# One 512-column matmul for both activation halves in the stages without meta tokens

## The chip, the cores and the metric

The kernel runs on one core of one Trainium2 chip. The metric is the device time of one execution in microseconds, the median over several runs. All arithmetic counts as float32: the answer has to hold float32 accuracy, and the kernel reaches that with matmuls of split operands, described below.

## What is computed

One encoder layer over 272 positions (16 learned meta tokens ahead of 256 real ones) of width 2048. It is a half-weighted SwiGLU, then a mixer whose single input projection feeds differential attention and a state-space scan, then an output projection, then a second half-weighted SwiGLU. The meta positions are dropped at the end, so everything behind the keys, the values and the scanned inputs is needed for the 256 real positions alone.

```
def _swiglu(h, w_gate, w_up, w_down):
    return (jax.nn.silu(h @ w_gate) * (h @ w_up)) @ w_down
...
        h = h + 0.5 * _swiglu(_rmsnorm(h, ffn1_norm[l]), ffn1_w_gate[l], ffn1_w_up[l], ffn1_w_down[l])
        u = _rmsnorm(h, mix_norm[l]) @ w_in[l]
...
        h = h + jnp.concatenate([attn, ssd.astype(attn.dtype)], axis=-1) @ w_out[l]
        h = h + 0.5 * _swiglu(_rmsnorm(h, ffn2_norm[l]), ffn2_w_gate[l], ffn2_w_up[l], ffn2_w_down[l])
    return h[:, N_META:]
```

## The kernel before

The residual stream stands transposed in SBUF, features on partitions, tokens along the row. Weights come in 648 tiles of 128 x 1024 float32 (512 KB) in the order of their use. ScalarE (ACT) rounds a tile to `hi` (L154), VectorE (DVE) makes the remainder `lo` (L156), both in the fp32r format that TensorE (PE) reads at one column a cycle. Four buffers hold split tiles; splitting runs three tiles ahead of use. The activations are split in the same way into `yh` and `yl` (or `gh`, `gl` inside the SwiGLU).

A product is three matmuls: `hi`x`yh` (L197), `hi`x`yl` (L198), `lo`x`yh` (L199), in the helper `mm3`, each of which loads its own stationary 128 x 128 weight block and streams the tokens past it. The three add up in the same columns of one PSUM bank. `project(t0)` makes four chunks of 128 output columns from eight weight tiles: per tile it goes through the four chunks, and in each through the tile's two blocks. With `t0 = 0` a matmul has 272 columns, with `t0 = META` it has 256.

Without meta tokens run: the gate and up projections of the second SwiGLU (22 calls of `project(META)`), the projections of the gate z and of the queries (two calls each) and the output projection `w_out_part` (eight groups of four weight tiles; the first four take the scan's half, the last four the attention's). The down projection of the second SwiGLU (`evac2`, L986 to L988) has the activations stationary and streams the weights, 512 columns in a matmul.

The results leave PSUM by an eviction behind each group. Five banks serve as `acc` tiles in turn, and a group takes four, so chunk c of a group stands in a bank until its eviction, and chunk c + 1 of the next group needs that bank. In the second SwiGLU the eviction of the gate is one DVE multiplication (L356), that of the up projection another (L366). Between the weight tiles `step()` and `need()` issue the rest of the mixer (norms, scan, attention) from a queue; a list scheduler then fixes each engine's order.

Of the kernel before, what the change touches and what calls it, by code (L numbers as in the profile page):

```python
# [17 lines left out]
P = 128  # L18
# [29 lines left out]
# columns of w_in  # L48
# [3 lines left out]
def _plan():  # L52
    """The weight tiles in the order of their use: (weight, first row, rows / 128, first column, columns)."""
# [26 lines left out]
# token tiles of the keys and of the scanned positions  # L80
# [4 lines left out]
def hymba_block(ctx: ExitStack, tc: tile.TileContext, h0, pars, consts, dtw, wts, out):  # L85
# [28 lines left out]
    class Lazy(dict):  # L114
        """Slots taken when first asked for."""
# [84 lines left out]

    def project(t0):
        """Four 128-column chunks of y @ w, transposed: [columns, tokens from t0]."""
        accs = [acc_tile() for _ in range(4)]
        for kt in range(KC // 2):
            hi, lo = wtile()
            for c in range(4):
                for k in range(2):
                    kc = 2 * kt + k
                    mm3(accs[c][:, 0:T - t0], hi[:, k, c * P:(c + 1) * P], lo[:, k, c * P:(c + 1) * P],
                        yh[:, kc, t0:T], yl[:, kc, t0:T], kc == 0, kc == KC - 1)  # L210
            step()
        return [a[:, 0:T - t0] for a in accs]

# [22 lines left out]
    # the clock of the tensor engine and the first table of the activation engine, before the data is there  # L236
# [6 lines left out]
    def pc(i):  # L243
        return pcol[:, i:i + 1]

# [1 line left out]
    yh = cp.tile([P, KC, T], F32R, name="yh")  # L247
    yl = cp.tile([P, KC, T], F32R, name="yl")
# [3 lines left out]
    def new_y(kc, wcol, t0, sums):  # L252
        """From the new chunk of h: the halves of h * w, and its share of the sum of squares."""
# [11 lines left out]
    def rsqrt(v, s, r):  # L265
        """r = 1 / sqrt(v): a first guess from the exponent's bits, then Newton steps; s is scratch, v is lost."""
# [8 lines left out]
    def rstd_of(v, width, r):  # L275
        """v: sums of squares, a column per tile of tokens; r = 1 / sqrt(mean + eps)."""
# [805 lines left out]
```

## Time and profile before

| | |
|---|---|
| time, median of 3 runs | 1986.74 us (1984.13 to 1987.38) |
| profiled execution, first to last instruction | 1980.9 us |
| median minus the profiled span | 5.8 us |
| PE busy | 1973.0 us, 15034 matmuls |
| DVE busy | 1103.0 us |
| ACT busy | 894.1 us |
| mean granted TensorE clock | 1.000 (2.4 GHz) |

The profile comes from one execution; of that one only the span is listed, and what lies around it is taken from the difference to the runs' median. PE's busy time counts a matmul from its start to its modelled end; neighbours overlap, so the pace of PE is read from start to start, not from the mean duration.

### The profile page before, as it was taken

The page shows a single profiled execution, that of the slowest core. Times are in us where ns is not written, and L with a number is a line of the kernel's source. Part 1 is how long each engine was busy: PE and PEld are TensorE (multiplying, and loading weights), DVE is VectorE, ACT ScalarE, POOL GpSimd, SP SyncE. Part 2 cuts the span into 40 slices and gives each one's busy share as a digit, 9 for nine tenths or more (in the row PEclk, how much of TensorE's full clock was granted, in tenths as well). Part 3 has the DMA queues.
Part 4 walks back from the last instruction along what each step waited for, and adds up shares of the span by engine and source line. Part 5 has one row for each costly group of instructions (what it writes and reads, how often), then busy time and mean ns, then how long its engine had stood idle before and what let it go on. Part 6 is the DMA issues. An engine that isn't in the chain of part 4 may idle for free.

```text
span 1980.9 us, 36104 instructions
## 1 busy us (share of the span) xinstructions
PE 1973.0 (100%) x15034; PEld 1904.1 (96%) x15034; DVE 1103.0 (56%) x1762; ACT 894.1 (45%) x1311; POOL 25.2 (1%) x61
## 2 busy tenths in 40 slices
PE   9999999999999999999999999999999999999999
PEld 9999999999999999999998889999999889999987
DVE  7545455454545456776866666555555544555554
ACT  6443443334343444456645665544444334444432
POOL 0000000000000000000021000000000000000000
PEclk9999999999999999999999999999999999999999
DMA  7455554544555555464465225455555555555563
GB/s 275 171 175 177 172 180 171 179 172 175 179 181 178 174 178 171 153 217 169 154 194 177 107 107 188 169 186 181 186 186 190 194 191 187 186 182 186 186 215 125
DMA packets 98324, 352.74 MB, mean 178 GB/s; under 512 B 11680, under 2 KB 11728, under 8 KB 98160
## 3 DMA queue, kind: packets, MB, share of 16 engines
q1 hardware_dynamic: 94464, 342.02, 49.5%
q0 software_dynamic: 2544, 6.33, 1.1%
q8 instruction: 117, 1.92, 0.4%
q10 hardware_dynamic: 1152, 2.10, 0.3%
q14 instruction: 47, 0.39, 0.1%
HBM read 347.18 MB, written 3.21 MB: 177 GB/s over the span
## 4 chain that ended last, share of the span: by engine, by line
PE 97%; DVE 1%; DMA 1%; ACT 1%; issue 0%; SPq 0%; POOL 0%; DVEq 0%; ACTq 0%
PE acc L197 27%; PE acc L199 27%; PE acc L198 27%; PE acc L987 4%; PE acc L988 4%; PE acc L986 4%; PE ps L743 1%; ACT hi L154 0%; PE ps L628 0%; DMA u<-k_d 0%; DVE lo L156 0%; DMA raw<-in_wts_dram 0%; PE ps L799 0%; PE ps L802 0%; PE ps L765 0%
## 5 line engine op out<-in xcount | busy, mean ns | idle before, releaser
L156 DVE TENSOR_TENSOR lo<-raw,hi 128x1024 fp32r<-128x1024 f32 x648 | 792.7, 1224 | 732.5 <-ACT hi L154 729.3
L154 ACT CAST hi<-raw 128x1024 fp32r<-128x1024 f32 x648 | 681.7, 1052 | 991.1 <-PE acc L198 770.0
L197 PE MATMUL acc<-yh,hi 128*128 128x272 f32 (+1 forms) x3520 | 1007.9, 286 | 0.8 <-DVE u L648 0.7
L199 PE MATMUL acc<-yh,lo 128*128 128x272 f32 (+1 forms) x3520 | 1001.7, 285 | 0.4 <-DVE lo L156 0.4
L198 PE MATMUL acc<-yl,hi 128*128 128x272 f32 (+1 forms) x3520 | 1001.2, 285 | 0.0
L197 PEld LDWEIGHTS acc<-yh,hi 128*128 128x128 f32 x3520 | 661.8, 188 | 5.0 <-issue 2.0
L199 PEld LDWEIGHTS acc<-yh,lo 128*128 128x128 f32 x3520 | 662.2, 188 | 2.2 <-issue 1.2
L198 PEld LDWEIGHTS acc<-yl,hi 128*128 128x128 f32 x3520 | 661.9, 188 | 1.6 <-issue 1.2
L199 PE MATMUL acc<-u,lo 128*128 128x272 f32 (+1 forms) x960 | 277.3, 289 | 0.0
L197 PE MATMUL acc<-u,hi 128*128 128x272 f32 (+1 forms) x960 | 277.2, 289 | 0.0
L198 PE MATMUL acc<-u,hi 128*128 128x272 f32 (+1 forms) x960 | 275.9, 287 | 0.0
L199 PEld LDWEIGHTS acc<-u,lo 128*128 128x128 f32 x960 | 181.8, 189 | 2.1 <-issue 1.4
L198 PEld LDWEIGHTS acc<-u,hi 128*128 128x128 f32 x960 | 181.8, 189 | 1.0 <-issue 0.4
L197 PEld LDWEIGHTS acc<-u,hi 128*128 128x128 f32 x960 | 181.5, 189 | 1.0 <-issue 0.4
L988 PE MATMUL acc<-lo,u 128*128 128x512 f32 x352 | 137.0, 389 | 0.0
L987 PE MATMUL acc<-hi,u 128*128 128x512 f32 x352 | 137.0, 389 | 0.0
L986 PE MATMUL acc<-hi,u 128*128 128x512 f32 x352 | 136.9, 389 | 0.0
L986 PEld LDWEIGHTS acc<-hi,u 128*128 128x128 f32 x352 | 66.1, 188 | 13.7
L987 PEld LDWEIGHTS acc<-hi,u 128*128 128x128 f32 x352 | 66.1, 188 | 13.7
L988 PEld LDWEIGHTS acc<-lo,u 128*128 128x128 f32 x352 | 66.1, 188 | 13.7
L366 DVE TENSOR_TENSOR u<-acc,u 128x272 f32<-128x272 f32 (+1 forms) x88 | 33.9, 427 | 30.9 <-PE acc L199 30.9
L356 DVE TENSOR_TENSOR u<-acc,rm 128x256 f32<-128x256 f32 (+1 forms) x84 | 33.1, 429 | 31.4 <-PE acc L199 31.4
(266 smaller groups left out, 708.8 us busy)
## 6 DMA issues: line engine op xcount, KB each, us to landing
raw<-in_wts_dram SPq DMA_DIRECT2D x648, 512.0 KB, 3.3
u<-a_d POOLq DMA_DIRECT2D x4, 512.0 KB, 7.7
out_dram<-hx ACTq DMA_DIRECT2D x8, 256.0 KB, 4.7
hx<-in_h_dram SPq DMA_DIRECT2D x7, 272.0 KB, 7.4
u<-k_d POOLq DMA_DIRECT2D x4, 272.0 KB, 7.5
u<-in_consts_dram POOLq DMA_DIRECT2D x1, 472.0 KB, 4.8
hx<-in_h_dram SPq DMA_DIRECT2D x1, 280.0 KB, 2.9
rope<-u POOLq DMA_DIRECT2D x4, 68.0 KB, 2.5
```

The lines of the kernel that those rows point to most:

```text
L154: nc.scalar.copy(hi, raw)
L156: nc.vector.tensor_tensor(lo, raw, hi.bitcast(F32), ALU.subtract)
L197: nc.tensor.matmul(ps, st_hi, mv_hi, start=first, stop=False)
L198: nc.tensor.matmul(ps, st_hi, mv_lo, start=False, stop=False)
L199: nc.tensor.matmul(ps, st_lo, mv_hi, start=False, stop=last)
L356: nc.vector.tensor_tensor(sg[:, c, :], pg[c], rm[:, t0:T], ALU.mult)
L366: nc.vector.tensor_tensor(sg[:, c, :], pu[c], sg[:, c, :], ALU.mult)
L743: nc.tensor.matmul(pss[s], qT[h // 4][r, h % 4, j * P:(j + 1) * P], kT[h // 4][r, h % 4, 0:kw], start=True, stop=True)
L986: nc.tensor.matmul(accs[j], a, hi[:, k, :], start=first, stop=False)
L987: nc.tensor.matmul(accs[j], b_, hi[:, k, :], start=False, stop=False)
L988: nc.tensor.matmul(accs[j], a, lo[:, k, :], start=False, stop=last)
```

## The change

Where there are no meta tokens, the halves `yh` and `yl` (one tile `y` of two rows for each block now; also `oo` and `zz` for the output projection) are streamed by one matmul of 512 columns against `hi`: columns 0 to 255 of the bank get `hi`x`yh`, columns 256 to 511 `hi`x`yl`. A second matmul adds `lo`x`yh` to the columns 256 to 511. The two halves of the bank are added when they are read: `join` copies the upper half to SBUF on ACT, and adds the lower half on DVE. What a DVE instruction did on reading the bank is now done behind it in SBUF. In the attention half of the output projection each half of the bank is added to the residual by its own DVE addition.

```
+    def mm2(ps, st_hi, st_lo, mv, first, last):
+        nc.tensor.matmul(ps, st_hi, mv, start=first, stop=False)
+        nc.tensor.matmul(ps[:, SEQ:2 * SEQ], st_lo, mv[:, 0, :], start=False, stop=last)
...
+                    if t0:
+                        mm2(accs[c], *w, y[:, kc, :, t0:T], kc == 0, kc == KC - 1)
+                    else:
+                        mm3(accs[c][:, 0:T], *w, yh[:, kc, :], yl[:, kc, :], kc == 0, kc == KC - 1)
...
+    def join(dst, ps):
+        nc.scalar.copy(dst, ps[:, SEQ:2 * SEQ])
+        nc.vector.tensor_tensor(dst, ps[:, 0:SEQ], dst, ALU.add)
...
-    yh = cp.tile([P, KC, T], F32R, name="yh")
-    yl = cp.tile([P, KC, T], F32R, name="yl")
+    y = cp.tile([P, KC, 2, T], F32R, name="y")
+    yh, yl = y[:, :, 0, :], y[:, :, 1, :]
...
+                if t0:
+                    for c in range(4):
+                        join(sg[:, c, :], pg[c])
+                        pg[c] = sg[:, c, :]
...
+                if t0:
+                    us = [row_tmp(SEQ) for _ in range(4)]
+                    for c in range(4):
+                        join(us[c], pu[c])
+                    pu = us
...
+        if wi == 0:
+            for c in range(4):
+                join(dst[g][:, c, :], pj[c])
...
-    zh, zl = Lazy([P, 4, SEQ], F32R), Lazy([P, 4, SEQ], F32R)
+    zz = Lazy([P, 2, 2, SEQ], F32R)
...
-                    mm3(accs[c][:, 0:SEQ], hi[:, k, c * P:(c + 1) * P], lo[:, k, c * P:(c + 1) * P],
-                        hs[i // 4][:, i % 4, :], ls_[i // 4][:, i % 4, :], i == 0, i == 7)
+                    mm2(accs[c], hi[:, k, c * P:(c + 1) * P], lo[:, k, c * P:(c + 1) * P],
+                        src[i // 2][:, i % 2], i == 0, i == 7)
...
-            nc.vector.tensor_tensor(t, accs[c][:, 0:SEQ], rz, ALU.mult)
+            join(t, accs[c])
             ts.append(t)
+        for t in ts:
+            nc.vector.tensor_tensor(t, t, rz, ALU.mult)
...
-            nc.vector.tensor_tensor(h, h, accs[c][:, 0:SEQ], ALU.add)
+            for k in range(2):
+                nc.vector.tensor_tensor(h, h, accs[c][:, k * SEQ:(k + 1) * SEQ], ALU.add)
```

The order of PE, first change: two blocks of one weight tile for one chunk, in the first tile of an up projection of the second SwiGLU, before.

```order
L197 MATMUL acc_14960<-yh,hi_14966 128x256
L198 MATMUL acc_14960<-yl,hi_14966 128x256
L199 MATMUL acc_14960<-yh,lo_14968 128x256
L197 MATMUL acc_14960<-yh,hi_14966 128x256
L198 MATMUL acc_14960<-yl,hi_14966 128x256
L199 MATMUL acc_14960<-yh,lo_14968 128x256
```

The same of the changed kernel (the numbers behind the names differ between the two programs).

```order
L204 MATMUL acc_13960<-y,hi_13988 128x512
L205 MATMUL acc_13960<-y,lo_13990 128x256
L204 MATMUL acc_13960<-y,hi_13988 128x512
L205 MATMUL acc_13960<-y,lo_13990 128x256
```

Six matmuls of 256 columns have become two of 512 and two of 256; the sequence of chunks and tiles is the same.

The order of DVE, second change: the end of that up projection before, where the four `acc` tiles are its four chunks in turn, L156 is the split of a weight tile, L366 reads the bank and L368 makes `gl`.

```order
L156 TENSOR_TENSOR lo_15148<-raw_15114,hi_15146 128x1024
L366 TENSOR_TENSOR u_14951<-acc_14960,u_14951 128x256
L156 TENSOR_TENSOR lo_15178<-raw_15144,hi_15176 128x1024
L368 TENSOR_TENSOR u_15205<-u_14951,u_15204 128x256
L366 TENSOR_TENSOR u_14951<-acc_14961,u_14951 128x256
L366 TENSOR_TENSOR u_14951<-acc_14962,u_14951 128x256
L366 TENSOR_TENSOR u_14951<-acc_14963,u_14951 128x256
L156 TENSOR_TENSOR lo_15226<-raw_15174,hi_15224 128x1024
```

The same place of the changed kernel; L227 is the addition of `join`, L390 the multiplication that was L366, now without a bank, L392 the former L368.

```order
L156 TENSOR_TENSOR lo_14122<-raw_14096,hi_14120 128x1024
L227 TENSOR_TENSOR t_14142<-acc_13960,t_14142 128x256
L227 TENSOR_TENSOR t_14143<-acc_13961,t_14143 128x256
L227 TENSOR_TENSOR t_14144<-acc_13962,t_14144 128x256
L390 TENSOR_TENSOR u_13943<-t_14142,u_13943 128x256
L390 TENSOR_TENSOR u_13943<-t_14143,u_13943 128x256
L390 TENSOR_TENSOR u_13943<-t_14144,u_13943 128x256
L227 TENSOR_TENSOR t_14145<-acc_13963,t_14145 128x256
L392 TENSOR_TENSOR u_14141<-u_13943,u_14140 128x256 x3
L390 TENSOR_TENSOR u_13943<-t_14145,u_13943 128x256
L156 TENSOR_TENSOR lo_14174<-raw_14118,hi_14172 128x1024
```

The read of the first chunk's bank has moved behind the weight split that it stood ahead of, and the three multiplications have come in between the reads of the third and of the fourth bank.

On ACT at that place of the changed kernel the copies of `join` (L226) stand between two roundings of weight tiles (L154); before there was no instruction of ACT that read these banks.

```order
L154 CAST hi_14120<-raw_14096 128x1024
L226 COPY t_14142<-acc_13960 128x256
L226 COPY t_14143<-acc_13961 128x256
L226 COPY t_14144<-acc_13962 128x256
L154 CAST hi_14172<-raw_14118 128x1024
L226 COPY t_14145<-acc_13963 128x256
L391 CAST u_14140<-u_13943 128x256 x3
```

Up to the projections without meta tokens (z, some 880 us into the run) the order of all matmuls is that of before.

## Rows read from the trace of the kernel before

**Rows 1.** The page: busy time by engine; granted clock by slice.

```profile
PE 1973.0 (100%) x15034; PEld 1904.1 (96%) x15034; DVE 1103.0 (56%) x1762; ACT 894.1 (45%) x1311; POOL 25.2 (1%) x61
...
PEclk9999999999999999999999999999999999999999
```

**Rows 2.** The page: chain of work that ended last, by engine.

```profile
PE 97%; DVE 1%; DMA 1%; ACT 1%; issue 0%; SPq 0%; POOL 0%; DVEq 0%; ACTq 0%
```

**Rows 3.** Waits of PE alone: total us, times, longest.

```profile
PE ps L239 <- DVE ones L216: 1.1, 1, 1.1
PE acc L197 <- DVE u L648: 0.7, 1, 0.7
PE acc L199 <- DVE lo L156: 0.4, 1, 0.4
```

**Rows 4.** Timeline of PE, 256 columns: first and last of 19 consecutive matmuls.

```profile
1700.08 0.29 PE L197 MATMUL acc<-yh,hi 128*128 128x256 f32 x1
...
1702.22 0.28 PE L197 MATMUL acc<-yh,hi 128*128 128x256 f32 x1
```

**Rows 5.** Timeline of PE, 272 columns: first and last of 19 consecutive matmuls.

```profile
600.03 0.29 PE L197 MATMUL acc<-yh,hi 128*128 128x272 f32 x1
...
602.29 0.29 PE L197 MATMUL acc<-yh,hi 128*128 128x272 f32 x1
```

**Rows 6.** Timeline of PE, 512 columns: first and last of 22 consecutive matmuls.

```profile
1515.05 0.39 PE L986 MATMUL acc<-hi,u 128*128 128x512 f32 x1
...
1519.81 0.39 PE L986 MATMUL acc<-hi,u 128*128 128x512 f32 x1
```

**Rows 7.** Windows of the second SwiGLU: us, busy by engine (count), clock, DMA, GB/s.

```profile
1250.00:1500.00 250.00, 250.00 (x2106) 250.00 (x2105) 129.20 (x152) 107.94 (x133) 0.00 (x0) 1.00 0.54 186
1520.00:1630.00 110.00, 110.00 (x487) 91.06 (x487) 53.49 (x47) 43.12 (x41) 0.00 (x0) 1.00 0.55 194
```

**Rows 8.** Groups by line and shape: matmuls of 256 columns (count, busy, mean ns).

```profile
L197 PE MATMUL acc<-yh,hi 128*128 128x256 f32 x1664 | 470.1, 283 | 0.0
L198 PE MATMUL acc<-yl,hi 128*128 128x256 f32 x1664 | 467.4, 281 | 0.0
L199 PE MATMUL acc<-yh,lo 128*128 128x256 f32 x1664 | 467.0, 281 | 0.0
...
L197 PE MATMUL acc<-u,hi 128*128 128x256 f32 x256 | 73.8, 288 | 0.0
```

**Rows 9.** Groups by line and shape: splits, evictions, and an ACT copy from PSUM.

```profile
L156 DVE TENSOR_TENSOR lo<-raw,hi 128x1024 fp32r<-128x1024 f32 x648 | 792.7, 1224 | 732.5 <-ACT hi L154 729.3 <-PE ps L784 1.8
...
L366 DVE TENSOR_TENSOR u<-acc,u 128x256 f32<-128x256 f32 x44 | 16.6, 419 | 15.2 <-PE acc L199 15.2
...
L942 DVE TENSOR_TENSOR hx<-hx,acc 128x256 f32<-128x256 f32 x16 | 6.1, 418 | 5.5 <-PE acc L199 5.5
...
L807 ACT COPY u<-ps 128x256 f32<-128x256 f32 x8 | 3.0, 376 | 0.0
```

**Rows 10.** Timeline of DVE at the end of an up projection.

```profile
1278.68 0.42 DVE L366 TENSOR_TENSOR u<-acc,u 128x256 f32<-128x256 f32 x1 [1.38 <-PE acc L199]
1279.03 1.21 DVE L156 TENSOR_TENSOR lo<-raw,hi 128x1024 fp32r<-128x1024 f32 x1
1280.16 0.42 DVE L368 TENSOR_TENSOR u<-u,u 128x256 fp32r<-128x256 f32 x1
1280.49 1.08 DVE L366 TENSOR_TENSOR u<-acc,u 128x256 f32<-128x256 f32 x3
```

**Rows 11.** Timeline of ACT at the same place.

```profile
1277.85 1.05 ACT L154 CAST hi<-raw 128x1024 fp32r<-128x1024 f32 x1 [1.80 <-PE acc L198]
...
1280.75 1.05 ACT L154 CAST hi<-raw 128x1024 fp32r<-128x1024 f32 x1 [1.20 <-PE acc L198]
1281.71 1.01 ACT L367 CAST u<-u 128x256 fp32r<-128x256 f32 x3
```

**Rows 12.** Windows of the mixer, columns as in rows 7.

```profile
943.00:1000.00 57.00, 57.00 (x480) 53.08 (x479) 51.31 (x150) 39.09 (x100) 2.26 (x4) 1.00 0.45 153
...
1116.00:1128.00 12.00, 12.00 (x103) 12.00 (x103) 10.01 (x31) 7.54 (x16) 0.00 (x0) 1.00 0.48 177
...
1176.00:1190.00 14.00, 13.96 (x118) 13.75 (x117) 11.11 (x29) 8.96 (x17) 0.00 (x0) 1.00 0.34 122
```

**Rows 13.** Waits of all engines: those of the weight roundings for their transfers.

```profile
ACT hi L154 <- DMA raw<-in_wts_dram: 2.4, 6, 0.9
```

More of the change, by code (lines that the diff above doesn't have):

```diff
@@ L208, in project @@
                     kc = 2 * kt + k
-                    mm3(accs[c][:, 0:T - t0], hi[:, k, c * P:(c + 1) * P], lo[:, k, c * P:(c + 1) * P],
-                        yh[:, kc, t0:T], yl[:, kc, t0:T], kc == 0, kc == KC - 1)
+                    w = hi[:, k, c * P:(c + 1) * P], lo[:, k, c * P:(c + 1) * P]
+                    if t0:
+                        mm2(accs[c], *w, y[:, kc, :, t0:T], kc == 0, kc == KC - 1)
+                    else:
+                        mm3(accs[c][:, 0:T], *w, yh[:, kc, :], yl[:, kc, :], kc == 0, kc == KC - 1)
             step()
-        return [a[:, 0:T - t0] for a in accs]
+        return accs if t0 else [a[:, 0:T] for a in accs]
+    def join(dst, ps):
+        nc.scalar.copy(dst, ps[:, SEQ:2 * SEQ])
+        nc.vector.tensor_tensor(dst, ps[:, 0:SEQ], dst, ALU.add)
     ones = cp.tile([P, P], F32, name="ones")
@@ L644, in qk_evac @@
         sqs = []
+        if wi == 0:
+            for c in range(4):
+                join(dst[g][:, c, :], pj[c])
+            pj = [dst[g][:, c, :] for c in range(4)]
         for c in range(4):
-            sq = row_tmp(pj[c].shape[1])
-            nc.scalar.activation(sq, pj[c], AF.Square)
-            nc.vector.tensor_scalar(dst[g][:, c, :], pj[c], pc(R_QN + wi), None, ALU.mult)
+            p = pj[c]
+            sq = row_tmp(p.shape[1])
+            nc.scalar.activation(sq, p, AF.Square)
+            nc.vector.tensor_scalar(dst[g][:, c, :], p, pc(R_QN + wi), None, ALU.mult)
             sqs.append(sq)
@@ L818, in o_norm @@
                 nc.scalar.activation(O[g][:, j, c, :], O[g][:, j, c, :], AF.Copy, scale=orr[:, 4 * j + c:4 * j + c + 1])
-    oh, ol = Lazy([P, 4, SEQ], F32R), Lazy([P, 4, SEQ], F32R)
+    oo = Lazy([P, 2, 2, SEQ], F32R)
     def o_turn(h):
@@ L826, in o_turn @@
             nc.tensor.transpose(ps[:, j * P:(j + 1) * P], O[g][:, j, c, :], ident)
-        a, b_ = oh[g][:, c, :], ol[g][:, c, :]
+        a, b_ = oo[h // 2][:, h % 2, 0, :], oo[h // 2][:, h % 2, 1, :]
         nc.scalar.activation(a, ps[:, 0:SEQ], AF.Copy, scale=an8)
@@ L844, in attend, with z_a @@
             later(0.45, o_turn, h, label=f"o{h}")
-    zh, zl = Lazy([P, 4, SEQ], F32R), Lazy([P, 4, SEQ], F32R)
+    zz = Lazy([P, 2, 2, SEQ], F32R)
     zss = cp.tile([P, SEQ], F32, name="zss")
     zs = Lazy([P, 4, SEQ])
-    def z_a(ps, ch):
+    def z_a(ch):
         t = zs[ch // 4][:, ch % 4, :]
-        nc.vector.tensor_tensor(t, ps, rm[:, META:T], ALU.mult)
+        nc.vector.tensor_tensor(t, t, rm[:, META:T], ALU.mult)
         nc.scalar.activation(t, t, AF.Silu)
@@ L860, in z_b @@
         nc.vector.tensor_tensor(t, t, xs[g][:, c, META:T], ALU.mult)
-        a, b_ = zh[g][:, c, :], zl[g][:, c, :]
+        a, b_ = zz[ch // 2][:, ch % 2, 0, :], zz[ch // 2][:, ch % 2, 1, :]
         nc.scalar.activation(a, t, AF.Copy, scale=pc(R_SSD + ch))
@@ L873, in hymba_block @@
         for c in range(4):
-            z_a(pj[c], 4 * g + c)
+            join(zs[g][:, c, :], pj[c])
+        for c in range(4):
+            z_a(4 * g + c)
     later(2.4, ssd_exp, 0)
@@ L911, in hymba_block, with w_out_part @@
     zv, zr = small("zv", 2), small("zr", 2)
-    def w_out_part(hs, ls_):
+    def w_out_part(src):
         accs = [acc_tile() for _ in range(4)]
@@ L926, in hymba_block @@
     for dg in range(4):
-        accs = w_out_part(zh, zl)
+        accs = w_out_part(zz)
         need("rz")
@@ L938, in hymba_block @@
     for dg in range(4):
-        accs = w_out_part(oh, ol)
+        accs = w_out_part(oo)
         for c in range(4):
             h = hT[:, 4 * dg + c, META:T]
-            nc.vector.tensor_tensor(h, h, accs[c][:, 0:SEQ], ALU.add)
+            for k in range(2):
+                nc.vector.tensor_tensor(h, h, accs[c][:, k * SEQ:(k + 1) * SEQ], ALU.add)
         for c in range(4):
```

## The prediction

> **What bounds the kernel now.** I read the page's engine totals first: PE is busy all through, in all 40 slices at the full granted clock [rows 1]. The chain that ended last is 97% PE [rows 2]. So a nanosecond taken from PE's stream of matmuls comes off the end, and one added anywhere else costs only if PE comes to wait for it. The list of PE's own waits shows how little it waits: 1.1 us at the start, 0.7 us once for an eviction of the queries, 0.4 us once for a weight split [rows 3]. Neither bank releases nor weights hold it in the second SwiGLU.
>
> PE is not simply at one column per cycle, though. From start to start, 256 columns take (1702.22 - 1700.08) / 18 = 118.9 ns [rows 4], 272 columns 2.26 / 18 = 125.6 ns [rows 5], 512 columns 4.76 / 21 = 226.7 ns [rows 6]. At the granted 2.4 GHz the columns alone are 106.7, 113.3 and 213.3 ns. What is left over is 12.2, 12.2 and 13.3 ns: a price for each matmul that hardly depends on its size. Long stretches bear the two paces out: 250 us / 2106 = 118.7 ns and 110 us / 487 = 225.9 ns [rows 7].
>
> **The change, term by term.** There are 1664 + 256 = 1920 triples of 256 columns [rows 8]: 22 x 64 = 1408 in the second SwiGLU, 256 for z and q, 256 in the output projection. The columns streamed stay the same (768 a triple), but three matmuls become two.
>
> *Term 1, PE.* A triple takes 3 x 118.9 = 356.7 ns. As 512 + 256 it takes 226.7 + 118.9 = 345.6 ns. The difference is 11.1 ns, over 1920 triples 21.3 us. The one price in this that no row shows: for 1664 triples the 512 columns lie in two rows of 256 with 16 columns between them, while the matmuls of rows 6 read 512 in one piece (as `zz` and `oo` will). The lower bound is the 226.7 ns of one piece, the upper two matmuls of 256, 237.8 ns, at which those triples gain nothing and 2.8 us remain from the output projection. I take the lower end: rows 4 to 6 charge by the instruction and its columns, and this is one instruction of 512 columns. Both ends stay in the range.
>
> The Trainium skill, TensorE: Matmul & The Clock Gate, section "Wait — 56ns, not 53.3ns?", states a fixed cost of about 2.5 ns for a warm matmul. By that figure alone the estimate would be 1920 x 2.5 = 4.8 us instead of 21.3. The measured 12.2 ns disagrees with it, and the measurement decides.
>
> *Term 2, joins.* In 26 projections and four groups of the output projection each chunk gets an ACT copy and a DVE addition of 256 columns: 30 x 4 = 120 of each, priced by the ACT copy of that shape at 376 ns (45 us on ACT) and by DVE's eviction at 419 ns (50 us on DVE) [rows 9]. The attention half of the output projection gets 16 more DVE additions at 418 ns, 6.7 us. All of it lies beside PE: in the second SwiGLU's gate and up stretch DVE is busy 129.2 of 250 us and ACT 107.9 [rows 7]. Per projection of 22 us it adds 4 x 0.42 = 1.7 us to DVE and 4 x 0.38 = 1.5 us to ACT. I cost it at nothing there, if the banks come free in time.
>
> *Term 3, the banks.* That is the one wait that the change can create. Put 0 at the start of the weight rounding in the last tile of a projection (1277.85, when PE has let go of the tile before) [rows 11]. Before, the first chunk was read at 1278.68, so at +0.83 [rows 10]. In the new order rounding, copies, and on DVE split and additions follow each other. The split begins at +1.18 (1279.03) and the next DVE instruction at +2.31 (1280.16). The copies on ACT (from about +0.96, as 1281.71 follows 1280.75) hide under it. So the additions begin at +2.31 and, at a spacing of 1.08 / 3 = 0.36 and 0.42 each, let banks one to three go at about +2.7, +3.1 and +3.5. PE's tile takes 8 x 345.6 = 2.76 us; the next projection's second chunk, which needs bank one, starts at about 2.76 + 0.69 = +3.4, its third at +4.1, its fourth at +4.8. The margins are 0.7, 1.0 and 1.3 us. Bank four is not needed for another whole projection, so the rounding and the three multiplications ahead of its read cost nothing. The DVE split that now comes later (L156 behind ten short operations, about +6.5 instead of +5.2) is for a tile used at about 4 x 2.76 = +11.1. If the cover were gone, each us past the margin would cost 1 us at each of 22 projections.
>
> In the attention half of the output projection two additions for each bank put the first bank at about +2.9 and the second at +4.0, against the same +3.4 and +4.1: just in time, and four groups at 0.2 us are under 1 us. Around z, q and the scan's half of the output projection DVE is busy 51.3 of 57, 10.0 of 12 and 11.1 of 14 us [rows 12], with the scan and the attention in front of the evictions. There I bound the loss between 0 and 0.5 us at each of 8 groups, so 0 to 4 us. The 0.7 us wait of rows 3 stays about as it is: the queries' first three banks are now read ahead of the key scaling that held DVE, but the fourth chunk's squares stand behind it.
>
> *Term 4, the weights.* A tile is used up in 2.76 us instead of 2.85, so 190 GB/s. The down projection already draws 194 GB/s [rows 7], and in the whole run roundings waited 2.4 us for transfers [rows 13]. Nothing.
>
> *Sum.* 1980.9 - 21.3 + 1.0 (for term 3) = 1960.6 us of span. What lies around the span is taken as unchanged, 5.8 us between this span and the median of the three runs; so 1966.4 us, 1.0% less.
>
> **The rivals.**
> *A. The two-row read is charged as two reads.* For it: no row shows such a read. Against it: the price per matmul is the same from 256 to 512 columns. It gives 1986.7 - 2.8 + 1 = 1985; a half charge 1976.
> *B. The price of a matmul is not saved in this mix.* A short matmul now stands between long ones, and if the price of a long one's stationary block fell on it, the pair would take 356.7 ns as the triple does: 1986.7 + 1 = 1988, and with a quarter of the gain 1982. Against it: the price neither grows nor shrinks from 256 to 512 columns [rows 4 to 6], so it goes with the instruction. The small fixed cost that the Trainium skill, TensorE: Matmul & The Clock Gate, states in the section named above would be a mild form of this case.
> *C. Banks are let go late, and the kernel gets slower.* The place is the second chunk of each of the 34 groups, with the join's addition behind the weight split on DVE. The gain per group is 21.3 / 34 = 0.63 us, so it decides from an eviction later by 0.7 + 0.63 = 1.3 us than worked out. One more weight split in front (1224 ns [rows 9]) leaves 34 x (1.22 - 0.7) = 18 us of waits, so 1983; two more leave 34 x (2.45 - 0.7) = 60 us, so 2025. For it: two engines in turn now free a bank, and splits of 1.2 us stand in the same queue. Against it: before, one split stood between the first and second eviction and nobody waited; the order shows one ahead of the additions now.
> *D. Half of the 34 waits of C appear* (scheduling in the mixer alone, and a little in the SwiGLU): 5 to 10 us lost, 1971 to 1976.
>
> **How the numbers follow.** The forecast case, 1962 to 1970, has 0.80. A with a full charge has 0.04, a partial charge 0.04 (1970 to 1980), B 0.03, C 0.04 (half of it slower, the mild half near 1983), D 0.05. The range 1961 to 1976 takes in the forecast, D and the milder part of A, about 0.88, which leaves some room for steps I missed. No change (within 0.2%, 4 us, about what a measurement of this kernel can tell from none) is full A, the full form of B and the mild part of C. So faster 0.91, same 0.06, slower 0.03.
>
> **What would show each step.** Right: matmuls of 512 columns from `y` follow each other with the one of 256 in 345 to 347 ns a pair; the stretch of gate and up projections in the second SwiGLU shrinks by 3.1%; PE's list of waits stays at a few us; everything up to 880 us stands as before. Wrong: pairs of about 357 ns (A or B); waits of PE for DVE's join, 22 or more times (C); the splits of weight tiles ahead of the joins twice in a row; ACT waiting for transfers. The prediction fails if the two-row read has a price of its own, or if the eviction by two engines reaches into the next group.

## The result and the profile after

The changed kernel takes 1975.18 us (median of 5 runs, 1972.9 to 1979.66), the kernel before 1984.13 us beside it (5 runs, 1983.34 to 1987.38); the ratio is 0.9948, 95% interval 0.9936 to 0.996. That is 9 us less, inside the range of 1961 to 1976 but at its upper end, and under half of the 20 us forecast. The profiled execution took 1974.47 us with a span of 1972.7, against 1980.9 before: 8.2 us to explain, where 20.3 were worked out.

The page of the changed kernel, busy time by engine and granted clock by slice (as [rows 1]):

```profile
PE 1960.8 (99%) x13114; PEld 1804.7 (91%) x13114; DVE 1142.3 (58%) x1898; ACT 927.3 (47%) x1431; POOL 25.3 (1%) x61
...
PEclk9999999999999999999999999999999999999999
```

1920 matmuls are gone and PE is still busy all through, so the time has to be looked for in PE's own pace and in a few waits. Its waits (total us, times, longest; as [rows 3]):

```profile
PE acc L204 <- DVE t L227: 1.8, 1, 1.8
PE ps L686 <- ACT t L676: 1.7, 1, 1.7
PE ps L254 <- DVE ones L231: 1.1, 1, 1.1
PE acc L197 <- ACT hi L154: 0.8, 1, 0.8
```

Both at the top stand in the mixer. The first is new; at the place of the second PE waited 0.7 us before, for the eviction of the queries [rows 3]. L204 and L205 are the two matmuls of a pair, L226 and L227 the copy and the addition of `join`. Windows of the changed kernel, each cut from the first matmul of a stretch to the first of the next (us, busy by engine with counts, granted clock, DMA share, GB/s; a matmul that still runs at an edge is counted too): second gate and up sweep of the second SwiGLU, z, the queries, the values, the scan's half and the attention's half of the output projection:

```profile
1635.51:1859.51 224.00, 224.00 (x1282) 195.74 (x1280) 127.67 (x172) 107.65 (x155) 0.00 (x0) 1.00 0.58 188
883.57:932.97 49.40, 49.40 (x295) 43.16 (x293) 39.78 (x102) 32.18 (x59) 0.00 (x0) 1.00 0.50 171
990.87:1040.08 49.21, 48.94 (x293) 40.66 (x292) 34.37 (x79) 24.19 (x40) 11.40 (x20) 1.00 0.66 201
1040.08:1113.19 73.11, 71.39 (x501) 62.22 (x499) 42.65 (x124) 41.64 (x117) 5.01 (x9) 1.00 0.48 145
1113.19:1185.85 72.66, 70.46 (x379) 55.36 (x377) 51.15 (x170) 47.24 (x135) 0.00 (x0) 0.98 0.33 104
1185.85:1232.03 46.18, 46.18 (x267) 40.10 (x265) 38.26 (x74) 25.62 (x41) 0.00 (x0) 1.00 0.58 189
```

The same stretches of the kernel before, in the same order:

```profile
1639.49:1867.71 228.22, 228.22 (x1921) 228.21 (x1920) 117.10 (x137) 96.69 (x117) 0.00 (x0) 1.00 0.53 185
883.73:933.96 50.23, 50.23 (x422) 49.61 (x421) 38.48 (x99) 31.70 (x55) 0.00 (x0) 1.00 0.50 168
991.81:1041.61 49.80, 49.63 (x421) 47.24 (x420) 33.51 (x73) 22.85 (x35) 11.40 (x20) 1.00 0.64 200
1041.61:1113.80 72.19, 71.46 (x500) 62.31 (x499) 42.36 (x121) 40.53 (x113) 5.00 (x9) 1.00 0.44 146
1113.80:1184.06 70.26, 70.13 (x509) 62.09 (x508) 49.29 (x164) 43.78 (x124) 0.00 (x0) 1.00 0.31 112
1184.06:1230.77 46.71, 46.71 (x393) 46.71 (x392) 32.37 (x52) 25.14 (x39) 0.00 (x0) 1.00 0.52 182
```

The first gate and up sweep, before and after:

```profile
1230.77:1508.89 278.12, 278.00 (x2342) 277.79 (x2341) 144.66 (x186) 127.43 (x170) 0.00 (x0) 1.00 0.52 182
1232.03:1504.93 272.90, 272.90 (x1575) 238.78 (x1573) 158.75 (x233) 141.00 (x217) 0.00 (x0) 1.00 0.57 186
```

Stretch by stretch, the balance in us is this.

| stretch | forecast | measured | short by |
|---|---|---|---|
| gate and up, both sweeps (1408 pairs) | -15.6 | -5.2 - 4.2 = -9.4 | 6.2 |
| z and queries (256) | -2.8 | -0.8 - 0.6 = -1.4 | 1.4 |
| output projection (256) | -2.8 | +2.4 - 0.5 = +1.9 | 4.7 |
| values | 0 | +0.9 | 0.9 |
| term 3's allowance | +1.0 | (in the rows above) | -1.0 |

Together 12.2 us; missing are 20.3 - 8.2 = 12.1. Two things want an explanation. A pair in the second SwiGLU takes 224.00 / 640 = 350.0 ns, not 345.6; and the output projection became slower.

### The profile page after: what moved, and what is told of

Read it like the earlier page. It is cut to its first block, busy times and chain, and to the rows that moved or that the text cites. A ratio compares the mean times of both kernels' runs of the same rounds, so it can differ in the third digit from the quotient of the medians.

```text
span 1972.7 us, 32522 instructions
## 1 busy us (share of the span) xinstructions
PE 1960.8 (99%) x13114; PEld 1804.7 (91%) x13114; DVE 1142.3 (58%) x1898; ACT 927.3 (47%) x1431; POOL 25.3 (1%) x61
## 4 chain that ended last, share of the span: by engine, by line
PE 97%; DMA 1%; DVE 1%; ACT 0%; issue 0%; POOL 0%; SPq 0%; ACTq 0%; DVEq 0%
PE acc L204 22%; PE acc L198 16%; PE acc L199 16%; PE acc L197 16%; PE acc L205 11%; PE acc L1022 4%; PE acc L1021 4%; PE acc L1020 4%; PE ps L772 1%; PE ps L652 0%; DMA u<-k_d 0%; DMA raw<-in_wts_dram 0%; DVE lo L156 0%; DMA k_d<-t 0%; ACT hi L154 0%
## 5 line engine op out<-in xcount | busy, mean ns | idle before, releaser
L156 DVE TENSOR_TENSOR lo<-raw,hi 128x1024 fp32r<-128x1024 f32 x648 | 792.2, 1223 | 712.3 <-ACT hi L154 709.2
L154 ACT CAST hi<-raw 128x1024 fp32r<-128x1024 f32 x648 | 680.0, 1050 | 952.2 <-PE acc L198 457.8
L204 PE MATMUL acc<-y,hi 128*128 128x512 f32 x1664 | 584.8, 396 | 0.0
L198 PE MATMUL acc<-y,hi 128*128 128x272 f32 x1856 | 536.9, 289 | 0.0
L197 PE MATMUL acc<-y,hi 128*128 128x272 f32 x1856 | 535.2, 288 | 0.9 <-ACT hi L154 0.8
L199 PE MATMUL acc<-y,lo 128*128 128x272 f32 x1856 | 535.2, 289 | 0.5 <-DVE lo L156 0.5
L205 PE MATMUL acc<-y,lo 128*128 128x256 f32 x1664 | 466.2, 280 | 0.0
L204 PEld LDWEIGHTS acc<-y,hi 128*128 128x128 f32 x1664 | 312.6, 188 | 74.1 <-issue 0.8
L197 PEld LDWEIGHTS acc<-y,hi 128*128 128x128 f32 x1856 | 350.0, 189 | 4.0 <-issue 1.1
L199 PEld LDWEIGHTS acc<-y,lo 128*128 128x128 f32 x1856 | 349.8, 189 | 1.9 <-issue 0.7
L198 PEld LDWEIGHTS acc<-y,hi 128*128 128x128 f32 x1856 | 349.7, 188 | 1.5 <-issue 1.2
L205 PEld LDWEIGHTS acc<-y,lo 128*128 128x128 f32 x1664 | 313.5, 188 | 0.0
L199 PE MATMUL acc<-u,lo 128*128 128x272 f32 x704 | 203.9, 290 | 0.0
L197 PE MATMUL acc<-u,hi 128*128 128x272 f32 x704 | 203.4, 289 | 0.0
L198 PE MATMUL acc<-u,hi 128*128 128x272 f32 x704 | 202.6, 288 | 0.0
L198 PEld LDWEIGHTS acc<-u,hi 128*128 128x128 f32 x704 | 132.9, 189 | 0.0
L197 PEld LDWEIGHTS acc<-u,hi 128*128 128x128 f32 x704 | 132.5, 188 | 0.0
L204 PE MATMUL acc<-u,hi 128*128 128x512 f32 x256 | 94.4, 407 | 1.8 <-DVE t L227 1.8
```

The source lines that it names most:

```text
L154: nc.scalar.copy(hi, raw)
L156: nc.vector.tensor_tensor(lo, raw, hi.bitcast(F32), ALU.subtract)
L197: nc.tensor.matmul(ps, st_hi, mv_hi, start=first, stop=False)
L198: nc.tensor.matmul(ps, st_hi, mv_lo, start=False, stop=False)
L199: nc.tensor.matmul(ps, st_lo, mv_hi, start=False, stop=last)
L204: nc.tensor.matmul(ps, st_hi, mv, start=first, stop=False)
```

## The experiments

**How fast can a pair be? Matmuls alone.** Two kernels without the block, in which one function streams 128 pairs or triples a stretch from one array `m`; the stretches differ in how the moving columns lie. `off` is the byte, counted from a multiple of 256, at which the first block begins (called its place from here on; the addresses are those of the program's allocation), `r` the distance of the two rows and `q` that of the blocks in columns. A has the layout of the changed kernel, whose blocks stand at places 224 and 96 in turn; D, E, F read 512 contiguous columns; in H and I all blocks stand at one place, 96 or 224; G has its rows 64 columns apart, at place 64; J and K are triples; L and N are matmuls of 512 alone, contiguous and from two rows; M and Q have two long matmuls and then the two short ones. 576 columns are 9 x 256 bytes, so they keep the place; 544 columns shift it by 128 bytes.

```
    def run(v, kind, off, r, q, n=2):
...
    run("A", "pair", 96, 272, 544)
    run("B", "pair", 64, 272, 544)
    run("C", "pair", 0, 272, 544)
    run("D", "pair", 32, 256, 512)
    run("E", "pair", 64, 256, 512)
    run("F", "pair", 0, 256, 512)
    run("G", "pair", 64, 320, 640)
    run("H", "pair", 96, 272, 576)
    run("I", "pair", 224, 272, 576)
    run("J", "triple", 96, 272, 544)
    run("K", "triple", 64, 256, 512)
    run("L", "long", 64, 256, 512)
    run("M", "two", 64, 256, 512)
    run("N", "long", 96, 272, 544)
    run("Q", "two", 96, 272, 544)
```

> This kernel leaves the block out: it only streams matmuls from one array, 128 pairs or triples a stretch, with the other engines idle. Three theories of why a pair took 350.0 ns in the second SwiGLU and not the forecast 345.6. Layout: a pair from two rows with 16 columns between them takes 350, one from 512 contiguous columns 346 to 347. Place: the pair's time follows the byte at which the moving rows begin, so stretches of the same shape that begin 96, 64 or 0 bytes past a multiple of 256 differ by some 5 ns, and the two stretches with a constant place give 347 and 353. Mix: a short matmul between long ones costs 4 ns more whatever the layout, so every stretch of pairs shows about 350, and two long ones followed by two short ones show 346 a pair or less. Triples: 356 to 360 ns in all theories; matmuls of 512 alone 226.7.

Windows of the run with the other engines idle, in the order A, E, H, I, J, K, L, N, Q; all but Q from the first matmul of a stretch to that of the next, so 128 pairs or triples each (L and N: 256 matmuls); Q's holds 63 groups of four:

```profile
81.25:126.05 44.80, 44.80 (x258) 39.15 (x257) 1.27 (x8) 0.00 (x0) 0.00 (x0) 1.00 0.00 1
260.86:306.08 45.22, 45.22 (x258) 39.19 (x257) 1.27 (x8) 0.00 (x0) 0.00 (x0) 1.00 0.00 1
396.52:440.90 44.38, 44.38 (x259) 39.29 (x257) 1.27 (x8) 0.00 (x0) 0.00 (x0) 1.00 0.00 1
440.90:486.13 45.23, 45.23 (x258) 39.69 (x257) 1.27 (x8) 0.00 (x0) 0.00 (x0) 1.00 0.00 1
486.13:531.35 45.22, 45.22 (x386) 45.22 (x385) 1.27 (x8) 0.00 (x0) 0.00 (x0) 1.00 0.01 1
531.35:577.43 46.08, 46.08 (x386) 46.08 (x385) 1.27 (x8) 0.00 (x0) 0.00 (x0) 1.00 0.00 1
577.43:635.49 58.06, 58.06 (x259) 48.05 (x257) 1.27 (x8) 0.00 (x0) 0.00 (x0) 1.00 0.00 1
680.06:739.38 59.32, 59.32 (x259) 48.08 (x257) 1.26 (x8) 0.00 (x0) 0.00 (x0) 1.00 0.00 1
739.38:783.06 43.68, 43.68 (x253) 38.49 (x252) 1.11 (x7) 0.00 (x0) 0.00 (x0) 1.00 0.00 1
```

Divided by 128: A 350.0 ns a pair, E 353.3, H 346.7, I 353.4; triples J 353.3, K 360.0; L 226.8 and N 231.7 a matmul (divided by 256); Q 43.68 / 126 = 346.7 a pair (the 345.8 of the expectation written for it further down was read between unequal points). So A repeats the 350.0 of the real kernel with nothing else going on, H and I split it into 346.7 and 353.3 by place alone, and the contiguous E is no better. B and C, whose blocks take turns between 64 and 192 and between 0 and 128, take 350.0 like A; D and F, contiguous, 353.2 and 353.4 like E; G 353.2; M 348.2. Layout (contiguous or not) falls as a theory of the pairs; place stands for pairs from two rows with 16 columns between them; mix, in its plain form, falls, since pairs of the same mix take 346.7, 350.0 and 353.3. One stretch does show a price of two rows: in N a matmul of 512 takes 4.9 ns more than in L, with no short matmul between.

> The same stretches as in the run with idle engines, while ScalarE and VectorE round and split weight tiles and the transfers run, as in the kernel. A fourth theory, traffic: the other engines' accesses to SBUF lengthen the matmuls; then each pace is some ns above that of the quiet run. If the matmuls keep their own pace, both runs agree within 1 ns.

Stretch A of that run:

```profile
80.21:125.02 44.81, 44.81 (x259) 39.16 (x258) 25.09 (x29) 21.48 (x21) 0.00 (x0) 1.00 0.75 241
```

With ScalarE, VectorE and the transfers at work, A takes 44.81 / 128 = 350.1 and K's uninterrupted stretches 360.0 again: traffic falls too. One thing was new. E, at 353.3 in the quiet run, was interrupted by waits here, and between them ran at another pace. PE's timeline, first and last of 59 pairs' long matmuls:

```profile
304.61 0.40 PE L144 MATMUL accE<-m,hi 128*128 128x512 f32 x1
...
324.72 0.40 PE L144 MATMUL accE<-m,hi 128*128 128x512 f32 x1
```

20.11 / 58 = 346.7 ns, at the same addresses. G went the same way: 346.7 ahead of an interruption in this run, 353.2 behind it. H and I kept their 346.7 and 353.3. So for contiguous columns, and for rows 64 columns apart, the same addresses allow either pace, and it changed at interruptions alone. That the way in which a stream is entered decides is the likely reading; no run tests it by itself.

**The second SwiGLU from contiguous columns.**

```diff
+    y2 = y.rearrange("p k s t -> p (k s t)")[:, 0:KC * 2 * SEQ].rearrange("p (k s t) -> p k s t", k=KC, s=2)
...
-                        mm2(accs[c], *w, y[:, kc, :, t0:T], kc == 0, kc == KC - 1)
+                        mm2(accs[c], *w, y2[:, kc] if last[0] else y[:, kc, :, t0:T], kc == 0, kc == KC - 1)
```

(`last` is set for the second SwiGLU, and `new_y` writes to `y2` there.)

> For the second SwiGLU the activations lie as 512 contiguous columns for each block. Layout: a pair takes 346.5 instead of 350.0 ns, 1408 x 3.5 = 4.9 us less than the changed kernel, 1970.3 us. Place: every block now begins 96 bytes past a multiple of 256, the place of the faster pairs, and the time is the same, 1970.3. Mix or traffic: no change, 1975.2.

Its second gate and up sweep, window from the first matmul to the end:

```profile
1631.18:1855.18 224.00, 224.00 (x1281) 195.17 (x1280) 127.68 (x172) 107.68 (x155) 0.00 (x0) 1.00 0.59 188
```

224.00 us, 350.0 ns a pair, to the digit as in the changed kernel. The layout theory falls in the real kernel too. Place is not tested by this run as its expectation says: the array's base had been miscounted, and the contiguous blocks all begin at place 160, not 96. The time is 1973.5 us (1970.17 to 1974.72, ratio 0.9939, 0.9926 to 0.9951), not told from the changed kernel; the shorter span of the profiled execution comes from the mixer (below).

**The place of the two rows, alone.** The blocks of the second SwiGLU lie 576 columns apart, first so that all begin at place 96, then at 224:

```diff
+    ybuf = cp.tile([P, KC * 576 + 64], F32R, name="y")
...
+    y2 = ybuf[:, 48:48 + KC * 576].rearrange("p (k c) -> p k c", k=KC)[:, :, 0:2 * T]
+    y2 = y2.rearrange("p k (s t) -> p k s t", s=2)[:, :, :, 0:SEQ]
```

The second kernel has 16 in place of 48 and nothing else.

> Only for the second SwiGLU, the blocks of activations lie 576 columns apart instead of 544, still in two rows with 16 columns between them, so that each block's moving rows begin 96 bytes past a multiple of 256 (in the changed kernel the blocks alternate between 96 and 224). Place: every pair takes 346.7 ns as in the stretch H of the quiet run, 1408 x 3.3 = 4.7 us less in the gate and up projections (492.2 instead of 496.9 us). If the place has no say in the real kernel, 350.0 ns and no change.

> The same layout, shifted so that each block's moving rows begin 224 bytes past a multiple of 256. Place: every pair takes 353.3 ns as in stretch I, 4.7 us more than the changed kernel in the gate and up projections (501.6 us), 9.4 us more than with place 96. If the place has no say, the same as with place 96.

Second gate and up sweep with place 96:

```profile
1629.98:1851.87 221.89, 221.89 (x1281) 196.59 (x1280) 127.69 (x172) 107.66 (x155) 0.00 (x0) 1.00 0.60 190
```

The same sweep with place 224:

```profile
1635.66:1861.79 226.13, 226.13 (x1282) 198.56 (x1281) 128.00 (x172) 107.56 (x155) 0.00 (x0) 1.00 0.59 187
```

221.89 / 640 = 346.7 ns and 226.13 / 640 = 353.3 ns, as foretold from H and I. The kernels take 1967.94 us (1966.83 to 1970.53, ratio 0.9907, 0.9892 to 0.9921) and 1978.31 us (1976.21 to 1980.25, 0.9959, 0.9945 to 0.9974): 10.4 us between two kernels that differ in 128 bytes of an address. In the two profiled runs both sweeps together take 492.3 and 501.5 us, so they hold 9.2 us of the difference.

**Another order of the four matmuls.**

```diff
-                        mm2(accs[c], *w, y[:, kc, :, t0:T], kc == 0, kc == KC - 1)
...
+                for k in range(2 * (t0 > 0)):
+                    kc = 2 * kt + k
+                    nc.tensor.matmul(accs[c], hi[:, k, c * P:(c + 1) * P], y[:, kc, :, t0:T], start=kc == 0, stop=False)
...
+                        nc.tensor.matmul(accs[c][:, SEQ:2 * SEQ], w[1], y[:, kc, 0, t0:T], start=False, stop=kc == KC - 1)
```

> In the projections without meta tokens the two matmuls of 512 columns of a weight tile's two blocks come first and then the two of 256, instead of 512, 256, 512, 256; layout as in the changed kernel. From stretch Q of the quiet run (345.8 ns a pair against A's 350.0): 1664 x 4.2 = 7.0 us less than the changed kernel, of it 5.9 in the second SwiGLU. If only the place counts, 350.0 and no change.

```profile
1636.99:1863.13 226.14, 226.14 (x1282) 196.36 (x1280) 128.07 (x172) 107.89 (x156) 0.00 (x0) 1.00 0.58 187
```

That window is once more the second gate and up sweep: 353.3 ns a pair, 1978.39 us (1978.04 to 1984.97, ratio 0.9972, 0.9954 to 0.9989). A miss, and in the wrong direction: the 346.7 of stretch Q did not carry over. One thing differs: Q's first block stands at place 96 and its second at 224, in the real kernel it is the other way round. For A the two come to the same cycle of pairs; here they do not (long at 96, long at 224, short at 96, short at 224 in Q; long at 224, long at 96, short at 224, short at 96 here). Whether that makes the difference was not tested, and it stays open.

**The layout without the matmuls.** Of the whole change only this, in the kernel before:

```diff
-    yh = cp.tile([P, KC, T], F32R, name="yh")
-    yl = cp.tile([P, KC, T], F32R, name="yl")
+    y = cp.tile([P, KC, 2, T], F32R, name="y")
+    yh, yl = y[:, :, 0, :], y[:, :, 1, :]
```

> The kernel before, with nothing of the change but the layout: both halves of a block lie next to each other as in the changed kernel, and three matmuls of 256 columns read them. Place: as in stretch J of the quiet run 353.3 ns a triple instead of 356.7, 1664 x 3.3 = 5.5 us less than before, 1980. If only the number of matmuls counts, 356.7 and the time of before.

Its second gate and up sweep:

```profile
1636.71:1862.84 226.13, 226.13 (x1921) 226.13 (x1920) 116.95 (x137) 96.25 (x117) 0.00 (x0) 1.00 0.55 187
```

226.13 / 640 = 353.3 ns a triple against 228.22 / 640 = 356.6 before, with every matmul of before still there. The kernel takes 1980.31 us (11 runs, 1976.9 to 1982.89, ratio 0.9973, 0.9964 to 0.9982). Both sweeps together take 506.3 us before, 501.8 with the layout alone (the first one 275.64) and 496.9 in the changed kernel. Half of what the change won in the second SwiGLU is won by moving the two halves next to each other; the smaller number of matmuls brings the other half. The move also changes the places at which the blocks begin, and the run does not separate the two.

**The output projection.** At 1175 us PE stood still for 1.78 us and then ran at the lower clock. PE there, in the changed kernel (timeline):

```profile
1173.58 0.48 PE L831 MATMUL ps<-u,wt 16*128 16x128 f32 x2
1175.85 0.50 PE L204 MATMUL acc<-u,hi 128*128 128x512 f32 x1 [1.78 <-DVE t L227]
```

ScalarE at that place:

```profile
1174.10 0.28 ACT L835 ACTIVATE t<-ps 128x128 f32<-128x128 f32 x1 [1.17 <-PE ps L831]
...
1174.62 0.37 ACT L836 COPY u<-ps 128x256 f32<-128x256 f32 x1
1174.87 1.49 ACT L226 COPY t<-acc 128x256 f32<-128x256 f32 x5
```

VectorE at that place:

```profile
1174.76 0.23 DVE L841 TENSOR_SCALAR ofin<-osq,lthr 128x8 f32<-128x8 f32 x1 [2.99 <-ACT t L835]
...
1175.37 1.41 DVE L227 TENSOR_TENSOR t<-acc,t 128x256 f32<-128x256 f32 x4
```

The join's copies (L226) stand on ScalarE behind the squares and the copy of the last attention head (L835, L836), which wait for PE's L831. PE's next matmul needs a bank that only these copies and the additions behind them set free. The additions stand on VectorE behind L841, which waits for the same squares. Before, VectorE alone read these banks (L932), ahead of the attention's work:

```profile
1171.10 1.41 DVE L932 TENSOR_TENSOR t<-acc,rz 128x256 f32<-128x256 f32 x4
```

Windows of the clock behind it:

```profile
1177.00:1178.00 1.00, 1.00 (x5) 0.90 (x4) 1.00 (x4) 0.00 (x0) 0.00 (x0) 0.50 0.09 25
1178.00:1179.00 1.00, 1.00 (x4) 0.81 (x4) 1.00 (x4) 0.00 (x0) 0.00 (x0) 0.50 0.00 0
1179.00:1180.00 1.00, 1.00 (x5) 0.90 (x4) 0.62 (x4) 0.95 (x1) 0.00 (x0) 0.50 0.00 0
```

A granted clock of 0.50 is 1.2 GHz. With the edges (0.93 in the microsecond ahead of these, 0.86 in the one behind) that makes some 3.4 us, in which a pair takes 0.64 us instead of 0.35: about 1.6 us lost. The wait of 1.8 us is in every run that keeps the join there (the place kernels, contiguous, other order); the fall of the clock behind it is not (1.00 in the window 1160 to 1180 with place 96 and contiguous, 0.91 with place 224, 0.84 with the other order). Two ways round the copies:

```diff
-                    mm2(accs[c], hi[:, k, c * P:(c + 1) * P], lo[:, k, c * P:(c + 1) * P],
-                        src[i // 2][:, i % 2], i == 0, i == 7)
...
+                    if src is zz:
+                        mm3(accs[c][:, 0:SEQ], *w, v[:, 0, :], v[:, 1, :], i == 0, i == 7)
...
-            join(t, accs[c])
+            nc.vector.tensor_tensor(t, accs[c][:, 0:SEQ], rz, ALU.mult)
```

> The scan's half of the output projection goes back to three matmuls and one VectorE read of each bank; everything else stays changed. If that half lost its time by banks that were let go late (a wait of 1.8 us and the lower clock behind it), the output projection takes about 116.1 us instead of 118.84: 112 x 6.7 ns less than the 117.0 of before; the kernel 1972.5. If the loss is the attention half's, it stays at 118 to 119 and the kernel at 1975 or above.

Its scan's half of the output projection:

```profile
1112.68:1182.94 70.26, 70.12 (x510) 62.09 (x508) 49.31 (x164) 43.66 (x124) 0.00 (x0) 1.00 0.34 113
```

70.26 us as before, no wait of PE for a bank and the full clock; the projection takes 115.3 us and the kernel 1970.71 (1968.97 to 1975.07, ratio 0.993, 0.9918 to 0.9942). Of the 3.5 us that the projection wins against the changed kernel, 1.1 come from the attention's half (45.1 against 46.18), in which nothing was edited. The two paces of contiguous columns show there. These are 80 pairs of that half, first in the changed kernel, then in the run with the contiguous second SwiGLU, where this half has the same instructions at the same addresses:

```profile
1199.17:1227.43 28.26, 28.26 (x163) 24.50 (x162) 23.18 (x41) 15.36 (x23) 0.00 (x0) 1.00 0.56 183
1195.40:1223.13 27.73, 27.73 (x162) 24.26 (x161) 23.13 (x41) 15.36 (x23) 0.00 (x0) 1.00 0.57 181
```

A pair takes 353.3 ns in the one and 346.6 in the other; with three matmuls in the scan's half it is the faster pace. The other way keeps the pairs:

```diff
-            t = row_tmp(SEQ)
-            join(t, accs[c])
-            ts.append(t)
-        for t in ts:
-            nc.vector.tensor_tensor(t, t, rz, ALU.mult)
+            for k in range(2):
+                t = row_tmp(SEQ)
+                nc.vector.tensor_tensor(t, accs[c][:, k * SEQ:(k + 1) * SEQ], rz, ALU.mult)
+                ts.append(t)
```

> In the scan's half of the output projection the pairs stay, but VectorE alone reads both halves of each bank (two multiplications by rz, two additions to the residual), with no copy on ScalarE. If the wait of 1.8 us and the lower clock behind it came from the copies that stood behind the attention's work on ScalarE, both are gone and the output projection takes 115 to 116 us instead of 118.84; the kernel 1971.5. If it is the number of reads or VectorE's load, a wait of PE for a bank stays there and the time is 1974 or more.

The two halves of its output projection:

```profile
1113.76:1181.57 67.81, 67.81 (x379) 54.08 (x377) 53.24 (x172) 42.64 (x120) 0.00 (x0) 1.00 0.34 110
1181.57:1229.67 48.10, 47.00 (x267) 40.12 (x265) 40.88 (x88) 25.36 (x40) 0.00 (x0) 1.00 0.58 184
```

The scan's half now shows the gain of the pairs (67.81 against 70.26), with VectorE busier than ever (53.24 us) and PE never waiting: it was the copies' place on ScalarE, not VectorE's load. (Freed from the copies, VectorE's reads of the first three banks also stand ahead of the attention's instructions again; the run does not separate the two.) 1.1 us of waits appear in the attention's half instead; 115.9 in all, and 1972.46 us (1972.14 to 1973.7, ratio 0.9929, 0.9914 to 0.9944).

**The values, and putting it together.** Place 96 and three matmuls in the scan's half:

> Place 96 in the second SwiGLU together with three matmuls in the scan's half of the output projection. If the two causes are independent, their parts add up: gate and up stretches 270.3 and 221.8 us as with place 96 alone, the scan's half 70.3 as with three matmuls alone; against the changed kernel 4.6 + 2.4 = 7 us less, 1968 or a little below. If the wait at the join is only moved elsewhere, PE's list of waits shows it again and the time stays at that of place 96 alone.

1966.81 us (1965.49 to 1969.86, ratio 0.9911, 0.9898 to 0.9923). The stretches add up as expected: PE's list of waits has no bank of the output projection in it, the scan's half takes 70.25 us (1113.21 to 1183.46). The whole is not told from place 96 alone (1967.94, 1966.83 to 1970.53). Then 576 columns in all stages:

```diff
-    y = ybuf[:, 0:KC * 2 * T].rearrange("p (k s t) -> p k s t", k=KC, s=2)
+    y = ybuf[:, 0:KC * 576].rearrange("p (k c) -> p k c", k=KC)[:, :, 0:2 * T]
+    y = y.rearrange("p k (s t) -> p k s t", s=2)
```

> As before, and the blocks of activations lie 576 columns apart in the other stages too, so that the matmuls of 272 columns begin at places 160 and 224 alone instead of 160 and 32, 224 and 96. In the changed kernel those at 160 and 224 took 124.8 ns and those at 32 and 96 126.9. Place: 1856 triples x half of them x 6.3 ns = 5.8 us less up to the values' projection, less 0.9 us for the pairs of the gates z and the queries, which are now all at place 224: 1962 to 1963. If the place matters for pairs alone, the same as the run without it, or 0.9 us more.

1965.44 us (1964.1 to 1970.21, ratio 0.9909, 0.9894 to 0.9925), again not told from the run without it, so the profile has to decide. The direction holds for 272 columns, the size is half: the second gate and up sweep of the first SwiGLU goes from 240.03 (443.34 to 683.37) to 238.94 us (441.83 to 680.77), 375.0 to 373.3 ns a triple, not 3.1 less.

The last wait is that at the start of the values. VectorE in the changed kernel:

```profile
1043.37 1.29 DVE L759 TENSOR_TENSOR u<-u,u 128x1088 f32<-128x1088 f32 x1 [2.69 <-DMA u<-k_d]
1044.58 0.42 DVE L227 TENSOR_TENSOR u<-acc,u 128x256 f32<-128x256 f32 x1
```

The scaling of the keys (L759) waits for a transfer, and the fourth addition of the queries' join is queued behind it; the square of that chunk on ScalarE waits for the addition, PE for the square. Before, the square read its bank itself, and PE waited for a bank whose eviction stood behind the same scaling. How long that wait is hangs on when the transfer lands, and it varies without the change too; in the run with the layout alone, which has no join, PE's list has

```profile
PE acc L197 <- DVE u L648: 2.0, 1, 2.0
```

and the values take 73.42 us. From the start of the scaling to PE's next matmul there are 1.74 us before (1042.03 to 1043.77) and in that run, 2.13 in the changed kernel (1043.37 to 1045.50). That leaves some 0.4 us for the join; the 0.9 us between the two traces are not shown to be the change's. The last kernel queues the scaling later:

```diff
-            later(1.2, k_scale, 0)
-            later(1.2, k_scale, 1)
         else:
+            later(1.2, k_scale, 0)
+            later(1.2, k_scale, 1)
```

> The kernel with 576 columns everywhere, and the scaling of the keys, which waits for a transfer of the keys' factors, is queued behind the queries' projection instead of ahead of its last eviction. If the wait of PE for ScalarE at the start of the values' projection (1.7 us in the changed kernel, 0.2 to 2.9 in the runs since) comes from the join's last addition behind that scaling on VectorE, it is gone and the values' projection takes about 71.3 us instead of 72.9; the kernel 1964. If it comes from ScalarE's own queue, the wait stays.

The values' stretch without and with it, first the kernel with 576 columns everywhere:

```profile
1037.40:1110.31 72.91, 71.24 (x501) 62.08 (x500) 42.60 (x124) 41.64 (x117) 5.00 (x9) 1.00 0.47 146
```

And with the keys scaled later:

```profile
1037.26:1107.73 70.47, 70.44 (x501) 61.94 (x499) 42.67 (x124) 41.60 (x117) 5.00 (x9) 1.00 0.48 153
```

The wait is gone from PE's list; 0.45 of the 2.44 us come back in the queries' stretch ahead of it (49.33 to 49.78). The kernel takes 1961.38 us (1960.82 to 1962.03, 4 runs; before beside it 1985.54), ratio 0.9879, 0.9863 to 0.9896: quicker than both kernels.

## Why the prediction was right, and why its size was not

- **What bounds the kernel**: right. Every gain and loss found is in PE's pace or in a wait of PE; 1975.18 us lies in the range and the sign was that forecast. That it lies in the range is in part luck: the range was worked out from 1986.74 us, the kernel before took 1984.13 beside the changed one, and 1986.74 x 0.9948 = 1976.4 would have missed it. Of the signs named for the pair, neither came: it is neither at 345 to 347 nor at 357, and the two sweeps shrank by 1.9%, not 3.1%.
- **Term 1** is the step that was mis-sized: "A triple takes 3 x 118.9 = 356.7 ns. As 512 + 256 it takes 226.7 + 118.9 = 345.6 ns. The difference is 11.1 ns." Measured, the triple is 356.6 and the pair 350.0, a difference of 6.7 (9.4 us in the second SwiGLU). Both paces were taken for constants of the instruction. They are not: with contiguous blocks (stretch K; 120.0 ns a matmul in the output projection of before) a triple takes 360.0, in the layout of before 356.7, in that of the changed kernel 353.3; the pair takes 346.7, 350.0 or 353.3. From 360.0 to 346.7 it is 13.3 ns, the price that [rows 6] give one matmul. The old layout happened to be one step better than 360.0, the new pair one step worse than 346.7, and 13.3 - 3.3 - 3.3 = 6.7 was left. Had the rows that 118.9 is a mean of been looked at one by one, they would have given a hint: the matmuls of 256 columns from `yh` and `yl` follow each other at anything from 115 to 128 ns.
- **The price that no row showed**, the two-row read: in pairs the two-row read is not dearer than the contiguous one (A 350.0, E 353.3, the contiguous kernel 350.0), so its lower bound was the nearer one. Alone it is: N against L shows 4.9 ns for a matmul of 512. Rival B, and A as a charge of two reads, are out: with place 96 a two-row pair in the same mix takes 346.7. A part of A is not, since the same pair takes 353.3 at place 224. Its middle form (1976) and rival D were the only cases near the measured time, and they had little weight. "Both ends stay in the range" does not hold: the upper end is rival A's 1985, and the range ends at 1976.
- **The fixed price**: the Trainium skill, TensorE: Matmul & The Clock Gate, section "Wait — 56ns, not 53.3ns?", states a fixed cost of about 2.5 ns for a warm matmul. Stretches L and K show 226.8 - 213.3 = 13.5 and 120.0 - 106.7 = 13.3 ns with a new stationary block for each matmul. The measurement decides; no run here shows 2.5.
- **Term 2, the joins**: right in price and cover. The copies took 371 and 373 ns, the additions 416, and in the second SwiGLU none of them delays PE.
- **Term 3, the banks**: right for the second SwiGLU and the attention's half (no wait of PE for a bank). Too small in the mixer, where it was bounded by 0 to 4 us and taken as part of 1.0: the scan's half lost 3.8 us against the forecast of -1.4, 1.8 of it by one wait and about 1.6 by the clock behind it, for which the prediction had no term. Rival D names this place; its 5 to 10 us are more than was lost there. The prediction had looked for the wait on VectorE, behind a weight split or the scan; it came by ScalarE, whose copies stood behind the attention's.
- "The 0.7 us wait stays about as it is": not borne out, and not by the join alone. It became 1.7 where the squares wait for VectorE; in the runs with the join it lay between 0.2 and 2.9 us, and in the one with the layout alone, without a join, it was 2.0. It follows the transfer.
- **Term 4** and "everything up to 880 us stands as before": right (883.57 against 883.73).

Of the missing 12.2 us most is shown by taking the cause away. Place 96 gives back 4.6 of the 6.2 in the second SwiGLU; the other 1.6 are the 345.6 itself, a sum of two paces from different layouts, against 346.7. In the output projection the run with three matmuls in the scan's half gives back 2.4 there and 1.1 in the attention's half, together 3.5 of 4.7. At z and the queries the pace of 350.0 would make 256 x 4.4 ns = 1.1 of the 1.4, without a run of its own, and the 0.9 at the values is not shown to be the change's.

## What to carry to other kernels

A pace read from one stage holds for its own layout; before a price per instruction is multiplied by 1408, look whether it is the same for each block, and try the same stream from other addresses and with interruptions, which costs one small kernel; what that shows is to be tried in the real one, where one of the two orders tried here came out otherwise. An eviction that is split over two engines stands in two queues: read both at each place, for what the engine that is new there has ahead of it. A change of layout that comes with another change should be run by itself: here it was half of the gain in the second SwiGLU.

## What the runs showed of the hardware that had not been expected

- Most streams of matmuls with float32r operands settled at paces that are 3.33 ns a pair or triple apart: 346.7, 350.0, 353.3; 353.3, 356.7, 360.0. At 2.4 GHz that is 8 clock periods (3.33 x 2.4). Stretch M, at 348.2, lies between two of them.
- For two rows of 256 columns with 16 between them, the place of the block modulo 256 bytes decides: 96 gives 346.7, 224 gives 353.3, in the small kernel and in the real one. For contiguous blocks the same addresses gave 353.3 in one run and 346.7 in another, in the small kernel and in the attention's half of the output projection. The order 512, 512, 256, 256 gave 346.7 in the small kernel and 353.3 in the real one, where the two places follow each other the other way round. What in the chip does this was not found.
- Matmuls of 512 columns one after another took 231.7 ns from two rows with 16 columns between them and 226.8 from one piece.
- An idle time of PE of 1.8 us was followed by some 3.4 us at 1.2 GHz in the changed kernel, by a lower clock in the runs with place 224 and the other order too, and by none in two others with the same wait.
